# A hybrid decoder step: the samples' first state made in the conv stage, earlier inputs for the scan's first block, the Toeplitz table on other rows

## The chip, the cores and the metric

The kernel runs on one core of a Trainium2 chip. The metric is the device time of one execution in microseconds. The median of three runs stands for the kernel; durations of single steps come from one profiled execution. The engines are called PE (matmul, TensorE), DVE (VectorE), ACT (ScalarE), POOL (GpSimd) and SP (SyncE, which only issues transfers here); POOL issues transfers too.

## What is computed

One step of a two-layer decoder over 256 prompt positions and 8 samples, 264 columns (T) in all. Layer one is a gated short convolution, layer two an S5 state-space layer, and a final RMSNorm follows. In the second layer (D_INNER 4096 as 256 groups of 16, state of 64 complex numbers per group):

```python
proj = h @ w_in
u, z = jnp.split(proj, 2, axis=-1)
lam_bar = jnp.exp(lam * dt)
b_bar = ((lam_bar - 1.0) / lam)[..., None] * b_c
bu = jnp.einsum('tbgh,gph->tbgp', u_c, b_bar)
bu = bu.at[0].add(lam_bar * carry)      # carry: state from before
_, states = lax.associative_scan(_scan_combine, (a_elems, bu), axis=0)
y_c = jnp.real(jnp.einsum('ghp,tbgp->tbgh', c_c, states))
...
y = y + d_skip * uf
y = jax.nn.gelu(y)
y = y * jax.nn.sigmoid(y @ w_glu + b_glu)
out = (y * jax.nn.silu(z)) @ w_out
```

For the samples, `carry` is the given state, so their new state is lam_bar times it plus one `bu`. For the prompt it starts at zero. The new states are outputs.

## The kernel before

All large products run on PE as 640 **slots** of 24 matmuls: eight contraction tiles of 128 by three products. Weights and inputs are split in a high part (wh on ACT, L196; the input's s, L258) and a remainder (wl on DVE, L205; the input's l, L259); a slot computes wh·s, wh·l and wl·s (L230, L231, L233). Slots 0 to 255 are conv's input projection, 256 to 319 its output, 320 to 383 u and 384 to 447 z of the S5 layer, 448 to 575 the GLU, 576 to 639 the last projection. A weight load (raw, L187, on SP) serves two slots; there are three raw buffers, four of wh, three of wl.

The S5 layer works on four blocks q of 64 groups (GB), each in eight tiles of inputs, that is four pairs:

- In conv's stage `tables` and `table_chunks` build, for 32 chunks j, tables from lam, B and C: vt (inputs to states), yt (states to outputs) and tt (a small Toeplitz kernel that takes four positions' inputs straight to their outputs, with d_skip on its diagonal). They go to DRAM as vt_d, yt_d, tt_d. The narrow matmuls of tt are L644, its DVE steps L651 and L655.
- `v_proc` makes bu of a block with vt (L904) and loads the samples' states h0_d into the block's S. `scan_proc` then makes 63 scan steps (L942 to L947, five DVE operations of 128x64, four positions per step). While it scans, the flag `scanning` is set, and wl of slots in the S5 projection is cut into four pieces that stand between the steps' operations (L202, `pop_fill`). After the last step come five operations over 128x512, L956 to L964: lam_bar times the samples' states is added to their bu (`fin`).
- `tw_proc` makes the outputs of each pair: 32 matmuls with tt on the inputs (L1028) and 32 with yt on the states (L1032), a "table pair" below. ACT copies them to yo (L1042), ten transfers write yo to y_d, five on POOL and five on SP (L1050, L1053), SP loads them back as yb (L1056), and ACT makes the gelu (L1058). yb is the GLU's input; the four splits of a tile pair follow (L258, L259).
- `state_out` transposes the block's last states (L978) and writes them out, for the last block on SP ahead of the last yb load (L990, L992).

The GLU's first slots, 448 to 465, are three output pairs with contraction quarters 0 to 2, and 466 to 471 their last quarter. It needs the y of the last block, its last eight contraction tiles 24 to 31, from four pairs. 

The order on each engine is what a planner writes out: `run.go` goes slot by slot, runs `procs` (generators that wait whole slots, or `Lag` microseconds of a counted time, 2.7 per slot) and `sides` (DVE work, by a credit of microseconds per slot). `U_ST` is the lag from the write of u to its use, `tw_done` counts finished pairs and gates the reuse of buffers.

Of the kernel before, what the change touches and what calls it, by code (L numbers as in the profile page):

```python
# [21 lines left out]
NS = 8  # L22
# [102 lines left out]
def tile_hybrid_conv_s5_step(  # L125
# [37 lines left out]
    tt_d = dram.tile([KI, 128, 4, 64], F32, name="tt_d")  # L163
    bp_d = dram.tile([128, G, GS], F32, name="bp_d")
    cp_d = dram.tile([128, G, GS], F32, name="cp_d")
    h0_d = dram.tile([128, G // GB, NS // 2, GB, 2], F32, name="h0_d")
# [31 lines left out]
    def conv_l(i):  # L198
        if i < len(run.slots):
            m = run.slots[i]["m"]  # L200
            wls[i] = wsp.tile([128, 8, 128], F32R, name="wl", bufs=3)
            parts = (4 if scanning[0] else 2) if n_ssm <= i < n_glu else 1  # L202
# [204 lines left out]
    def second_stage():  # L407
# [24 lines left out]
    def tables(pr):  # L432

        lamT, Ft, dcol, msk, eye = (tabs[k] for k in ("lam", "F", "dcol", "msk", "eye"))
# [7 lines left out]
        dr = pr.tile([128, 2, GS], F32, name="dr")  # L442
        mq.dma_start(dr, d_skip.rearrange("o (j gl h) -> (o j) gl h", gl=2, h=GS))
        ev = ident.rearrange("p (a h s) -> p a s h", a=2, h=GS)
        P.tensor_copy(eye, ev[:, 0])
        yield 6
        V.tensor_tensor(eye, eye, ev[:, 1], op=add)
        V.tensor_reduce(msk, eye, axis=mybir.AxisListType.X, op=add)
        drr = pr.tile([128, 2, GS, LC], F32, name="drr")
        P.tensor_copy(drr, dr[:, :, :, None].to_broadcast([128, 2, GS, LC]))  # L450
# [5 lines left out]
        PE.transpose(ps[:, :128], drr.rearrange("j a h s -> j (a h s)"), ident)  # L456
        yield 1
        V.tensor_copy(dcol, ps[:, :128])
# [114 lines left out]
        for k in range(1, 5):  # L573
            yield from spread(lr[k], li[k], lamT[:, :, k - 1, :])
        P.tensor_copy(lam1, lamT[:, :, 0, :])
        P.tensor_copy(lam4, lamT[:, :, 3, :])
# [48 lines left out]

    def table_chunks(ck):

        lamT, Ft, dcol, msk, eye = (tabs[k] for k in ("lam", "F", "dcol", "msk", "eye"))
# [9 lines left out]
        def products(j, X0, Y, vt):  # L638
            mq.dma_start(yt_d[j], Y[:, :, 1:5, :])
            mq.dma_start(vt_d[j], vt)  # L640
            pk = pss.tile([128, 512], F32, name="ps_a")
            pkv = pk[:, :256].rearrange("p (q n) -> p q n", q=4)
            for g in range(8):
                PE.matmul(pkv[(g % 2) * 64:(g % 2) * 64 + 64, g // 2, :],  # L644
                          X0[:, g].rearrange("p h s -> p (h s)"),
                          Y[:, g, 0:4, :].rearrange("p s h -> p (s h)"), start=True, stop=True)
            return pkv

        def toeplitz(j, pkv):
# [12 lines left out]
        prev = None
        for j in range(KI):
# [21 lines left out]
            X0 = ck.tile([128, 8, GS, LC], F32, name="X0")  # L685
# [584 lines left out]
```

## Time and profile before

| | |
|---|---|
| median of 3 runs | 2063.71 us (2061.16 to 2063.89) |
| the profiled execution | 2066.43 us, span 2064.7 us |
| PE busy | 2028.7 us, 98% of the span |
| DVE busy | 1486.7 us, 72% |
| ACT busy | 945.9 us, 46% |
| POOL busy | 198.0 us, 10% |

A busy share is an average over stages. With PE busy for nearly the whole span, one reads where it waits and for whom, then looks at that place in the windows (busy time of each engine per stretch and PE's granted clock) and in the timelines (start and duration of each instruction; in square brackets the idle time ahead of it and what ended that).

### The profile page before, as it was taken

The numbers are of one execution on the slowest core, as the hardware profiler recorded it, in microseconds if no ns is written. First come the engines' busy times: TensorE is split into PE (matmuls) and PEld (weight loads), VectorE is DVE, ScalarE is ACT, GpSimd is POOL, SyncE is SP. The second block draws the span as 40 slices with busy tenths as digits, with TensorE's granted clock in tenths as the row PEclk, the third lists the DMA queues.
The fourth block names the chain that finished last, engine by engine and source line by source line (L and its number), as shares of the span: only waits on it lengthen the run. The fifth ranks groups of instructions, "written<-read, shape, count | busy, mean of one in ns | idle before, by whom it ended". The sixth has DMA issues, their size and how long they took to land. (4 is left out here: it accounts for less than half of the span.)

```text
span 2064.7 us, 44611 instructions
## 1 busy us (share of the span) xinstructions
PE 2028.7 (98%) x17844; PEld 2001.1 (97%) x17844; DVE 1486.7 (72%) x3818; ACT 945.9 (46%) x1417; POOL 198.0 (10%) x365
## 2 busy tenths in 40 slices
PE   9999999999999999999999999999889999999997
PEld 9999999999999999999999999999779999999997
DVE  6785557999999999655548989999835555566453
ACT  6447554444444444444443334444344444455443
POOL 2000000000000000000132252524110000000000
PEclk9999999999999999999999999999989999999998
DMA  8656777776776777766787788879566566655653
GB/s 271 195 186 202 233 233 219 212 216 200 237 215 204 230 219 214 233 202 194 214 275 233 225 244 279 267 240 298 164 184 194 187 191 196 194 186 184 195 179 108
DMA packets 445172, 441.36 MB, mean 214 GB/s; under 512 B 69914, under 2 KB 426252, under 8 KB 444428
## 3 DMA queue, kind: packets, MB, share of 16 engines
q1 hardware_dynamic: 427780, 395.62, 62.4%
q0 software_dynamic: 17152, 42.88, 6.5%
q8 instruction: 140, 2.29, 0.4%
q14 instruction: 68, 0.56, 0.1%
q10 hardware_dynamic: 32, 0.01, 0.0%
HBM read 391.42 MB, written 47.15 MB: 212 GB/s over the span
## 5 line engine op out<-in xcount | busy, mean ns | idle before, releaser
L230 PE MATMUL acc_ps<-s,wh 128*128 128x264 f32 x4544 | 1307.2, 288 | 10.1 <-ACT s L258 8.3
L233 PE MATMUL acc_ps<-s,wl 128*128 128x264 f32 x4528 | 1287.8, 284 | 4.2 <-DVE wl L205 4.2
L205 DVE TENSOR_TENSOR wl<-raw,wh 128x1024 fp32r<-128x1024 f32 (+2 forms) x960 | 826.1, 865 | 369.9 <-PE acc_ps L233 222.7
L196 ACT ACTIVATE wh<-raw 128x1024 fp32r<-128x1024 f32 x640 | 677.7, 1060 | 902.3 <-PE acc_ps L231 709.0
L230 PEld LDWEIGHTS acc_ps<-s,wh 128*128 128x128 f32 x4544 | 858.0, 189 | 17.2 <-ACT s L258 9.4
L231 PE MATMUL acc_ps<-s,wh 128*128 128x264 f32 x3072 | 870.7, 284 | 0.0
L233 PEld LDWEIGHTS acc_ps<-s,wl 128*128 128x128 f32 x4528 | 852.1, 188 | 6.2 <-DVE wl L205 6.1
L231 PEld LDWEIGHTS acc_ps<-s,wh 128*128 128x128 f32 x3072 | 579.3, 189 | 0.0
L231 PE MATMUL acc_ps<-l,wh 128*128 128x264 f32 x1472 | 421.2, 286 | 2.3 <-DVE l L259 2.2
L231 PEld LDWEIGHTS acc_ps<-l,wh 128*128 128x128 f32 x1472 | 278.7, 189 | 3.5 <-DVE l L259 3.5
L943 DVE STREAM_SHUFFLE S<-S 128x64 f32<-128x64 f32 x252 | 74.8, 297 | 0.0
L230 PE MATMUL acc_ps<-yb,wh 128*128 128x264 f32 x256 | 73.0, 285 | 0.0
L230 PE MATMUL acc_ps<-ya,wh 128*128 128x264 f32 x256 | 72.9, 285 | 0.0
L231 PE MATMUL acc_ps<-yb,wh 128*128 128x264 f32 x256 | 72.7, 284 | 0.0
L233 PE MATMUL acc_ps<-ya,wl 128*128 128x264 f32 x256 | 72.6, 284 | 0.0
L233 PE MATMUL acc_ps<-yb,wl 128*128 128x264 f32 x256 | 72.5, 283 | 0.0
L231 PE MATMUL acc_ps<-ya,wh 128*128 128x264 f32 x256 | 72.5, 283 | 0.0
L725 POOL MEMSET ue<- 128x2 f32 x32 | 4.0, 128 | 606.4 <-DVE cv L737 551.8
L947 DVE TENSOR_TENSOR S<-S,prod 128x64 f32<-128x64 f32 x252 | 55.9, 222 | 2.3
L942 DVE TENSOR_TENSOR prod<-S,lam 128x64 f32<-128x64 f32 x252 | 55.5, 220 | 1.9
L945 DVE TENSOR_TENSOR prod<-S,lam 128x64 f32<-128x64 f32 x252 | 56.9, 226 | 0.0
L944 DVE TENSOR_TENSOR S<-S,prod 128x64 f32<-128x64 f32 x252 | 56.3, 223 | 0.0
(321 smaller groups left out, 1791.0 us busy)
## 6 DMA issues: line engine op xcount, KB each, us to landing
raw<-in_conv_w_in_dram SPq DMA_DIRECT2D x127, 1024.0 KB, 6.3
raw<-in_ssm_w_in_dram SPq DMA_DIRECT2D x64, 1024.0 KB, 6.8
raw<-in_ssm_w_glu_dram SPq DMA_DIRECT2D x64, 1024.0 KB, 5.1
raw<-in_conv_w_out_dram SPq DMA_DIRECT2D x32, 1024.0 KB, 5.6
raw<-in_ssm_w_out_dram SPq DMA_DIRECT2D x32, 1024.0 KB, 5.2
yt_d<-Y SPq DMA_DIRECT2D x32, 256.0 KB, 7.1
vt_d<-vt SPq DMA_DIRECT2D x32, 256.0 KB, 6.9
vt<-vt_d POOLq DMA_DIRECT2D x16, 512.0 KB, 7.5
```

Of the source, the lines that this page charges most:

```text
L196: A.activation(whs[i], raws[i][:, :, m * 128:(m + 1) * 128], AF.Copy)
L205: run.fill(lambda k=k: V.tensor_tensor(wls[i][:, k], raws[i][:, k, m * 128:(m + 1) * 128], whs[i][:, k], op=sub))
L230: PE.matmul(ps, wh[:, k, :], H(kt), start=first, stop=False)
L231: PE.matmul(ps, wh[:, k, :], L(kt), start=False, stop=False)
L233: PE.matmul(ps, wl[:, k, :], H(kt), start=False, stop=last)
L725: P.memset(halves(0)[:, :, 0:1], 0.0)
L942: V.tensor_tensor(pr[:, 0], cur, a4[:, 0], op=mult)
L943: V.stream_shuffle(sh, cur, SWAP)
L944: V.tensor_tensor(nxt, nxt, pr[:, 0], op=add)
L945: V.tensor_tensor(pr[:, 1], sh, a4[:, 1], op=mult)
L947: V.tensor_tensor(nxt, nxt, pr[:, 1], op=add)
```

## The change

- `step_samples` runs in conv's stage, after the tables' constants. For each block it loads h0_d, multiplies by lam_bar (shuffle, two products, sum) and writes lh_d. `scan_proc` loads lh when a block's scan begins and does one addition after the last step.
- U_ST is 4 instead of 6, `tw_done` is set one slot earlier, a `yield 1` is gone from `v_proc`, and wl may be cut in four in the GLU too while the scan runs.
- The Toeplitz products of a chunk write groups of 32 rows. The kernel's 16 rows are kept once, with zeros behind them (kt); the Toeplitz form arises in the transfers to tt_d, which read overlapping windows of 64 from it, eight transfers per chunk on POOL instead of one on SP. The five DVE steps become two small ones and a copy on ACT. tt is loaded in pieces of 256 B instead of 1 KB. yt's rows run in reverse, so yo's rows and the lam table do too (not shown).

```diff
-    tt_d = dram.tile([KI, 128, 4, 64], F32, name="tt_d")
+    tt_d = dram.tile([KI, 8, GS, LC, 64], F32, name="tt_d")
...
+    lh_d = dram.tile([128, G // GB, NS // 2, GB, 2], F32, name="lh_d")
...
-            parts = (4 if scanning[0] else 2) if n_ssm <= i < n_glu else 1
+            parts = 4 if scanning[0] else 2 if n_ssm <= i < n_glu else 1
...
             if left[0] == 0:
+                yield from step_samples(pr)
...
+    def step_samples(pr):
+
+        shape = [128, NS // 2, GB, 2]
+        for q in range(NB):
+            gs = slice(q * GB, (q + 1) * GB)
+            bc = lambda k: lam1[:, k, None, gs, None].to_broadcast(shape)
+            h, hs = (pr.tile(shape, F32, name=f"bn{c}") for c in range(2))
+            mq.dma_start(h, h0_d[:, q])
+            yield 4
+            V.stream_shuffle(hs, h, SWAP)
+            yield 0.7
+            V.tensor_tensor(hs, hs, bc(1), op=mult)
+            yield 0.7
+            V.tensor_tensor(h, h, bc(0), op=mult)
+            yield 0.7
+            V.tensor_tensor(h, h, hs, op=add)
+            yield 0.7
+            mq.dma_start(lh_d[:, q], h)
+
...
+            pkv = pk[:, :128].rearrange("p (r n) -> p r n", r=2)
             for g in range(8):
-                PE.matmul(pkv[(g % 2) * 64:(g % 2) * 64 + 64, g // 2, :],
-                          X0[:, g].rearrange("p h s -> p (h s)"),
-                          Y[:, g, 0:4, :].rearrange("p s h -> p (s h)"), start=True, stop=True)
+                PE.matmul(pkv[(g % 4) * 32:(g % 4) * 32 + 32, g // 4, :],
+                          X0[:, g].rearrange("p d h -> p (d h)"),
+                          Y[:, g, 1:5, :].rearrange("p s h -> p (s h)"), start=True, stop=True)
             return pkv
 
         def toeplitz(j, pkv):
-            tt = ck.tile([128, 4, 64], F32, name="tt")
-            V.tensor_tensor(tt, eye.rearrange("p s h -> p (s h)")[:, None, :].to_broadcast([128, 4, 64]),
-                            dcol[:, 4 * j:4 * j + 4, None].to_broadcast([128, 4, 64]), op=mult)
-            yield 0.33
-            for s in range(LC):
-                V.scalar_tensor_tensor(tt[:, :, 16 * s:], pkv[:, :, :64 - 16 * s], msk[:, s:s + 1],
-                                       tt[:, :, 16 * s:], op0=mult, op1=add)
-                yield 0.35 - 0.07 * s
-            mq.dma_start(tt_d[j], tt)
-
+            kt = kts[j % 2]
+            for r in range(2):
+                V.scalar_tensor_tensor(kt[:, r, 48:64], eye, dcol[:, 2 * j + r:2 * j + r + 1], pkv[:, r, 48:64], op0=mult, op1=add)
+            A.activation(kt[:, :, 0:48], pkv[:, :, 0:48], AF.Copy)
+            yield 1
+            for g in range(4):
+                for r in range(2):
+                    w = kt[32 * g:32 * g + GS, r, 0:64]
+                    P.dma_start(tt_d[j, 4 * r + g],
+                                bass.AP(tensor=w.tensor, offset=w.offset, ap=[w.ap[0], [GS, LC], [1, 64]]))
+
+        kts = [ck.tile([128, 2, 112], F32, name=f"kt{i}") for i in range(2)]
+        for kt in kts:
+            P.memset(kt[:, :, 64:], 0.0)
         nxt = load(0)
         yield 3
...
-            X0 = ck.tile([128, 8, GS, LC], F32, name="X0")
-            A.activation(X0, X[:, :, :, 3:4].to_broadcast([128, 8, GS, LC]), AF.Copy)
+            X0 = ck.tile([128, 8, 2, GS], F32, name="X0")
+            A.activation(X0, X[:, :, None, :, 3].to_broadcast([128, 8, 2, GS]), AF.Copy)
...
             while q >= 2 and tw_done[0] < (q - 1) * TB // 2:
                 yield 1
             mq.dma_start(S[:, 0:NS // 2], h0_d[:, q])
-            yield 1
             v_done[0] = q + 1
 
     def v_evac(S, ps, g):
...
+            lh = sw.tile([128, NS // 2, GB, 2], F32, name="lh", tag="big", bufs=1)
+            mq.dma_start(lh, lh_d[:, q])
...
             fin = S[:, a:a + n8]
-            sh8 = sw.tile([128, n8, GB, 2], F32, name="sh8", tag="big", bufs=1)
-            bc = lambda h: lam1[:, h, None, gs, None].to_broadcast([128, n8, GB, 2])
-            V.stream_shuffle(sh8, S[:, 0:n8], SWAP)
-            yield 0.6
-            V.tensor_tensor(sh8, sh8, bc(1), op=mult)
-            yield 0.6
-            V.tensor_tensor(fin, fin, sh8, op=add)
-            yield 0.6
-            V.tensor_tensor(sh8, S[:, 0:n8], bc(0), op=mult)
-            yield 0.6
-            V.tensor_tensor(fin, fin, sh8, op=add)
+            V.tensor_tensor(fin, fin, lh, op=add)
             fin_done[0] = q + 1
...
-        so = sw.tile([128, 4, 2, SD], F32, name="so", tag="big", bufs=1)
+        so = sw.tile([128, 4, 2, SD], F32, name="so", bufs=1)
...
             tt = ss["sw"].tile([128, 2, 4, 64], F32, name="tt", bufs=T_BUFS)
-            sq.dma_start(tt, tt_d[two].rearrange("j p q n -> p j q n"))
+            sq.dma_start(tt, tt_d[two].rearrange("j (q g) h s n -> (g h s) j q n", g=2))
...
                 run.extra += 2.0
                 for g in range(2):
                     spawn(tw_evac(i, yo, g, ps[g]), 1)
-                yield 2
+                yield 1
                 tw_done[0] = i + 1
+                yield 1
         spawn(state_out(NB - 1, S), 2)
 
     def tw_evac(i, yo, p, ps):
...
-    V_BUFS, Y_POOL, U_ST = 2, 5, 6.0
+    V_BUFS, Y_POOL, U_ST = 2, 5, 4.0
```

Some places at which the order of instructions changes. On DVE, the end of the last block's scan; wl is a weight remainder, S1 the block's states. Before:

```order
L942 TENSOR_TENSOR prod_19974<-S1_12666,lam4_76 128x64
L943 STREAM_SHUFFLE S1_12666<-S1_12666 128x64
L944 TENSOR_TENSOR S1_12666<-S1_12666,prod_19974 128x64
L945 TENSOR_TENSOR prod_19974<-S1_12666,lam4_76 128x64
L947 TENSOR_TENSOR S1_12666<-S1_12666,prod_19974 128x64
L1093 TENSOR_TENSOR zt_19721<-zt_19721,yb32_12662 128x264
L205 TENSOR_TENSOR wl_19983<-raw_19763,wh_19940 128x1024
L956 STREAM_SHUFFLE sh8_20009<-S1_12666 128x512
L958 TENSOR_TENSOR sh8_20009<-sh8_20009,lam1_77 128x512
L205 TENSOR_TENSOR wl_20051<-raw_19846,wh_19981 128x1024
L960 TENSOR_TENSOR S1_12666<-S1_12666,sh8_20009 128x512
L962 TENSOR_TENSOR sh8_20009<-S1_12666,lam1_77 128x512
```

After, the same place:

```order
L964 TENSOR_TENSOR prod_19992<-S1_12828,lam4_76 128x64
L965 STREAM_SHUFFLE S1_12828<-S1_12828 128x64
L966 TENSOR_TENSOR S1_12828<-S1_12828,prod_19992 128x64
L967 TENSOR_TENSOR prod_19992<-S1_12828,lam4_76 128x64
L206 TENSOR_TENSOR wl_19959<-raw_19676,wh_19904 128x256
L969 TENSOR_TENSOR S1_12828<-S1_12828,prod_19992 128x64
L206 TENSOR_TENSOR wl_19959<-raw_19676,wh_19904 128x256
L976 TENSOR_TENSOR S1_12828<-S1_12828,lh_18473 128x512
L206 TENSOR_TENSOR wl_20004<-raw_19782,wh_19957 128x256 x4
```

The step now has quarters of wl in it, and one addition with lh follows where five wide operations did; before, 23 steps stood behind the first four GLU splits, after, 12.

On SP, the end of the last block: y_d are the pairs' outputs, yb their loads, so and sp the state outputs. Before:

```order
L187 DMA raw_20393<-in_ssm_w_glu_dram 128x8x256
L1056 DMA yb32_12662<-y_d_83 128x2x264
L1050 DMA y_d_83<-yo_20299 16x8x8
L1053 DMA y_d_83<-yo_20299 16x8x64 x4
L1050 DMA y_d_83<-yo_20395 16x8x8
L1053 DMA y_d_83<-yo_20395 16x8x64 x4
L1056 DMA yb32_12662<-y_d_83 128x2x264
L990 DMA out_4_dram<-sp_20463 64x64
L992 DMA out_6_dram<-so_20462 64x4x64 x2
L990 DMA out_5_dram<-sp_20463 64x64
L992 DMA out_7_dram<-so_20462 64x4x64 x2
L1056 DMA yb32_12662<-y_d_83 128x2x264
```

After:

```order
L188 DMA raw_20500<-in_ssm_w_glu_dram 128x8x256
L1063 DMA y_d_83<-yo_20394 16x8x8
L1066 DMA y_d_83<-yo_20394 16x8x64 x4
L188 DMA raw_20569<-in_ssm_w_glu_dram 128x8x256
L1069 DMA yb32_12824<-y_d_83 128x2x264
L188 DMA raw_20650<-in_ssm_w_glu_dram 128x8x256
L1002 DMA out_4_dram<-sp_20573 64x64
L1004 DMA out_6_dram<-so_20572 64x4x64 x2
L1002 DMA out_5_dram<-sp_20573 64x64
L1004 DMA out_7_dram<-so_20572 64x4x64 x2
L1069 DMA yb32_12824<-y_d_83 128x2x264
```

Two raw loads (for slots 470 and 472) now stand between the last pair's writes and its load; the state outputs are ahead of that load in both. The table pairs of this block stand ahead of slots 453, 455, 458 and 460 on PE now, before ahead of 458, 460, 464 and 466.

On POOL, conv's stage; ue is a channel tile with its halo. Before:

```order
L725 MEMSET ue_3585 128x2
L725 MEMSET ue_3630 128x2
L725 MEMSET ue_4165 128x2
L725 MEMSET ue_4204 128x2
L725 MEMSET ue_4790 128x2
L725 MEMSET ue_4842 128x2
```

After:

```order
L675 DMA tt_d_86<-kt0_4877 64x1x64 x8
L675 DMA tt_d_86<-kt1_4878 64x1x64 x8
L746 MEMSET ue_8647 128x2
L675 DMA tt_d_86<-kt0_4877 64x1x64 x8
L746 MEMSET ue_8707 128x2
L675 DMA tt_d_86<-kt1_4878 64x1x64 x8
```

Groups of eight transfers of the table now stand between the memsets of conv's channels.

## Rows read from the trace of the kernel before

**Rows 1.** PE's waits for other engines: us in total, times, longest.

```profile
PE acc_ps L230 <- ACT s L258: 8.3, 4, 2.6
PE ps_a L978 <- DVE prod L942: 0.8, 1, 0.8
```

**Rows 2.** Windows of 10 us, columns: us, each engine's busy time, PEclk, DMA share, GB/s.

```profile
1450.00:1460.00 10.00, 7.15 (x52) 6.52 (x53) 9.79 (x40) 4.12 (x7) 0.00 (x0) 1.00 0.44 149
...
1520.00:1530.00 10.00, 4.44 (x17) 3.25 (x15) 1.55 (x4) 3.87 (x11) 0.00 (x0) 0.58 0.42 99
```

**Rows 3.** PE timeline, slots 448, 458, 462, 463, 464, within 466, 467, 468.

```profile
1442.98 0.28 PE L230 MATMUL acc_ps<-s,wh 128*128 128x264 f32 x1
...
1485.64 0.59 PE L230 MATMUL acc_ps<-s,wh 128*128 128x264 f32 x1
...
1500.33 0.28 PE L230 MATMUL ps_a<-s,wh 128*128 128x264 f32 x1
...
1503.25 0.28 PE L230 MATMUL ps_a<-s,wh 128*128 128x264 f32 x1
...
1508.13 0.39 PE L230 MATMUL ps_a<-s,wh 128*128 128x264 f32 x1
...
1530.78 0.59 PE L230 MATMUL acc_ps<-s,wh 128*128 128x264 f32 x1 [2.61 <-ACT s L258]
...
1532.52 0.42 PE L230 MATMUL acc_ps<-s,wh 128*128 128x264 f32 x1
...
1536.68 0.29 PE L230 MATMUL acc_ps<-s,wh 128*128 128x264 f32 x1
```

**Rows 4.** DVE timeline at the last scan: quarter pieces, splits, whole piece, last step's end.

```profile
1425.04 0.22 DVE L942 TENSOR_TENSOR prod<-S,lam 128x64 f32<-128x64 f32 x1
...
1425.65 0.42 DVE L205 TENSOR_TENSOR wl<-raw,wh 128x256 fp32r<-128x256 f32 x1
...
1426.46 0.22 DVE L942 TENSOR_TENSOR prod<-S,lam 128x64 f32<-128x64 f32 x1
...
1439.27 1.46 DVE L259 TENSOR_TENSOR l<-yb,s 128x264 fp32r<-128x264 f32 x4
...
1440.65 1.22 DVE L205 TENSOR_TENSOR wl<-raw,wh 128x1024 fp32r<-128x1024 f32 x1
...
1443.67 1.46 DVE L259 TENSOR_TENSOR l<-yb,s 128x264 fp32r<-128x264 f32 x4
...
1483.61 0.43 DVE L1093 TENSOR_TENSOR zt<-zt,yb 128x264 f32<-128x264 f32 x1
```

**Rows 5.** ACT timeline: the last gelu.

```profile
1529.63 0.64 ACT L1058 ACTIVATE yb<-yb 128x528 f32<-128x528 f32 x1 [3.14 <-DMA yb<-y_d]
```

**Rows 6.** SP timeline: last y_d writes, state outputs, last yb load.

```profile
1518.42 3.64 SPq L1053 DMA_DIRECT2D y_d<-yo  x4
...
1522.79 0.50 SPq L990 DMA_DIRECT2D out_dram<-sp  x1
...
1526.81 0.41 SPq L1056 DMA_DIRECT2D yb<-y_d  x1
```

**Rows 7.** Groups by shape, DVE: busy, mean ns.

```profile
L956 DVE STREAM_SHUFFLE sh<-S 128x512 f32<-128x512 f32 x4 | 3.0, 742 | 0.0
```

**Rows 8.** PE timeline: one group of the table's narrow matmuls.

```profile
358.44 0.69 PE L644 MATMUL ps_a<-Y,X 128*64 128x64 f32 x16
```

**Rows 9.** Line L1053, ns min/median/max, its POOL half.

```profile
L1053 POOL DMA_DIRECT2D y_d<-yo x64: 531/531/548, 1202.6 to 1519.1; - x64
```

**Rows 10.** DMA issues: KB each, median us to landing.

```profile
uct<-u_d POOLq DMA_DIRECT2D x16, 256.0 KB, 6.0
tt<-tt_d POOLq DMA_DIRECT2D x16, 256.0 KB, 6.6
```

**Rows 11.** The page's costliest groups: conv's memset on POOL.

```profile
L725 POOL MEMSET ue<- 128x2 f32 x32 | 4.0, 128 | 606.4 <-DVE cv L737 551.8
```

More of the change, by code (lines that the diff above doesn't have):

```diff
@@ L412, in second_stage @@
         tabs["F"] = tb.tile([128, 2, 4, G], F32, name="Ft")
-        tabs["dcol"] = tb.tile([128, 128], F32, name="dcol")
-        tabs["msk"] = tb.tile([128, LC], F32, name="msk")
-        tabs["eye"] = tb.tile([128, LC, GS], F32, name="eye")
+        tabs["dcol"] = tb.tile([128, 64], F32, name="dcol")
+        tabs["eye"] = tb.tile([128, GS], F32, name="eye")
         pre_p = tc.tile_pool(name="pre", bufs=1)
@@ L432, in tables @@
     def tables(pr):
-        lamT, Ft, dcol, msk, eye = (tabs[k] for k in ("lam", "F", "dcol", "msk", "eye"))
+        lamT, Ft, dcol, eye = (tabs[k] for k in ("lam", "F", "dcol", "eye"))
         nt = lambda name: pr.tile([128, 2, SD], F32, name=name)
@@ L441, in tables @@
         mq.dma_start(ldr, log_dt.rearrange("o (a g) -> (o a) g", a=2))
[L442 to L450, printed above, removed]
+        dr = pr.tile([64, 4, GS], F32, name="dr")
+        mq.dma_start(dr, d_skip.rearrange("o (j g h) -> (o j) g h", g=4, h=GS))
+        yield 2
+        V.tensor_reduce(eye, ident.rearrange("p (a h) -> p h a", h=GS), axis=mybir.AxisListType.X, op=add)
+        drr = pr.tile([64, 4, 2, GS], F32, name="drr")
+        P.tensor_copy(drr, dr[:, :, None, :].to_broadcast([64, 4, 2, GS]))
         ps = pss.tile([128, 512], F32, name="ps_a")
@@ L455, in tables @@
         ps = pss.tile([128, 512], F32, name="ps_a")
-        PE.transpose(ps[:, :128], drr.rearrange("j a h s -> j (a h s)"), ident)
+        PE.transpose(ps[:, :64], drr.rearrange("j g d h -> j (g d h)"), ident[:64, :64])
         yield 1
-        V.tensor_copy(dcol, ps[:, :128])
+        V.tensor_copy(dcol, ps[:, :64])
         M = 12582912.0
@@ L573, in tables @@
         for k in range(1, 5):
-            yield from spread(lr[k], li[k], lamT[:, :, k - 1, :])
-        P.tensor_copy(lam1, lamT[:, :, 0, :])
-        P.tensor_copy(lam4, lamT[:, :, 3, :])
+            yield from spread(lr[k], li[k], lamT[:, :, 4 - k, :])
+        P.tensor_copy(lam1, lamT[:, :, 3, :])
+        P.tensor_copy(lam4, lamT[:, :, 0, :])
         for k in range(4):
@@ L624, in state_layout @@
             mq.dma_start(h0_d[:, 2 * a2:2 * a2 + 2], ho)
+    def step_samples(pr):
[15 more added lines that the diff above has]
+            mq.dma_start(lh_d[:, q], h)
     def table_chunks(ck):
-        lamT, Ft, dcol, msk, eye = (tabs[k] for k in ("lam", "F", "dcol", "msk", "eye"))
+        lamT, Ft, dcol, eye = (tabs[k] for k in ("lam", "F", "dcol", "eye"))
         full = [128, 8, LC, GS]
@@ L691, in table_chunks @@
             Y = ck.tile([128, 8, 5, GS], F32, name="Y", bufs=2)
-            A.activation(Y[:, :, 0, :], cp, AF.Copy)
-            V.tensor_tensor(Y[:, :, 1:5, :], tab(lamT, 0), row(cp), op=mult)
+            A.activation(Y[:, :, 4, :], cp, AF.Copy)
+            V.tensor_tensor(Y[:, :, 0:4, :], tab(lamT, 0), row(cp), op=mult)
             yield 0.6
@@ L697, in table_chunks @@
             yield 0.6
-            V.tensor_tensor(Y[:, :, 1:5, :], Y[:, :, 1:5, :], m, op=sub)
+            V.tensor_tensor(Y[:, :, 0:4, :], Y[:, :, 0:4, :], m, op=sub)
             yield 0.6
@@ L1049, in tw_evac @@
             dq = P if 5 * jj < Y_POOL else mq
-            dq.dma_start(rows[:, :, NP:], yo[a:a + GS, :, 0:NS])
+            dq.dma_start(rows[:, :, NP:], yo[a + 3 * GS:a + 4 * GS, :, 0:NS])
             for s in range(LC):
                 dq = P if 5 * jj + s + 1 < Y_POOL else mq
-                dq.dma_start(rows[:, :, s * NCH:(s + 1) * NCH], yo[a + s * GS:a + (s + 1) * GS, :, Z:Z + NCH])
+                dq.dma_start(rows[:, :, s * NCH:(s + 1) * NCH], yo[a + (3 - s) * GS:a + (4 - s) * GS, :, Z:Z + NCH])
         yield Lag(Y_ST)
@@ L1087, in glu_in @@
         yield 1
-        sz = ss["sw"].tile([128, T], F32, name="sz", tag="sz" if j < 2 else "tt", bufs=1 if j < 2 else None)
+        sz = ss["sw"].tile([128, T], F32, name="sz", tag="so" if j < 2 else "tt", bufs=1 if j < 2 else None)
         A.activation(sz, zt, AF.Sigmoid)
```

3 lines of the change are left out of this document (1 added, 2 removed).

## Prediction

> **What bounds the kernel now.** I read the page's busy table first: TensorE (PE) is busy nearly all the time, so only time in which PE stands still, or runs at its lower clock, can be won. The list of PE's waits comes second. Its longest entry is the matmuls of L230 that wait for ACT's split of a GLU input [rows 1], all in one place. The table of windows shows what that place looks like: from 1450 to 1460 PE has 7.15 of 10 us with DVE at 9.79, and from 1520 to 1530 PE has 4.44 of 10 us at a granted clock of 0.58, that is between its two levels, 1.2 and 2.4 GHz, after it had stood still [rows 2]. PE's timeline gives the size. An ordinary slot of 24 matmuls takes 1503.25 - 1500.33 = 2.92 us, one with a table pair (L1028, L1032) 1508.13 - 1503.25 = 4.88 us, so the pair is 1.96 us [rows 3]. Slots 448 to 467, the start of the GLU, take 1536.68 - 1442.98 = 93.70 us [rows 3]; twenty slots and four pairs would take 58.4 + 7.8 = 66.2 us. The 27.5 us between are what the change can reach, and they lie in two parts:
>
> - **Scan part**, slots 448 to 457, 1485.64 - 1442.98 = 42.66 us for ten slots and one pair (31.2 us): 11.5 us too much. DVE is the late engine. A round of it (four splits, one weight remainder wl, two scan steps) takes 1443.67 - 1439.27 = 4.40 us against PE's 2.92 [rows 4].
> - **Tail part**, slots 458 to 467, 1536.68 - 1485.64 = 51.04 us for ten slots and three pairs (35.1 us): 15.9 us too much, of which I put 0.6 down to the five transposes of state_out, an estimate from the pair's 1.96 us for 64 matmuls; they stand in both kernels. Here PE waits at slot 466 for the outputs of the last four pairs: yo to y_d, back as yb, through the gelu on ACT. The last gelu waited 3.14 us for the transfer yb<-y_d [rows 5]. That load was issued at 1526.81, behind y_d writes from 1518.42 and the state outputs from 1522.79 on the same queue [rows 6].
>
> **The change part by part.**
>
> *lam_bar times the samples' states.* Per block, five DVE operations of 128x512 (0.742 us for the shuffle [rows 7]) become one; four at 0.74 at most are 3.0 us per block that leave DVE. Four sets of shuffle, two products and a sum go to the conv stage, as do a load of h0_d and a write of lh_d for each on SP; the block then loads lh, 256 KB, on SP. In conv, PE waits for neither DVE nor ACT for longer than the list's small entries, so these 4 x 3.0 = 12 us of DVE lie under PE; without that cover they would cost up to 12 us. At the earlier blocks the add frees state_out sooner: the 0.8 us for which PE waited at L978 [rows 1] goes.
>
> *Sooner inputs.* U_ST goes from 6 to 4, tw_done is set a slot earlier and a yield is gone. By the order of the changed kernel the scan of the last block moves forward against the slots: from the first four splits on, 23 scan steps were left, now 12. The last pairs stand at slots 453, 455, 458 and 460 (before 458, 460, 464, 466). So a pair's result has six slots more before slot 466 needs it.
>
> *Scan part.* The new rounds still hold four splits and one wl, now as four quarters between two steps. Two steps with quarters take 2 x (1426.46 - 1425.04) = 2.84 us and the four splits 1440.65 - 1439.27 = 1.38 [rows 4], so a round is 4.22 us. Six rounds are 25.3 us, against 1483.61 - 1439.27 = 44.3 us from the first four splits to the end of the last step, where the next operation starts [rows 4]: 19.0 us earlier on DVE. But the first pair stands five slots, 14.6 us, earlier on PE. The wait shrinks by 19.0 - 14.6 = **4.4 us**. Bounds: if the four quarters cost their full 0.42 us each in place of the whole piece's 1.22 [rows 4], a round would be 4.40 + 1.68 - 1.22 = 4.86 us, six 29.2, and 15.1 - 14.6 = 0.5 us is won; if the wait vanished, 11.5. I take 4.4, since the steps with quarters were timed in the same scan.
>
> *Tail part.* Let T be the start of slot 466. The pairs are done by slot 460, so all four y_d writes are out before T. What is late next is SP's queue: after raw(472), which waits for wl(467) and thus for PE's end of slot 464 (T - 2.9, plus 1.2 for wl), stand the state outputs, 1526.81 - 1522.79 = 4.0 us [rows 6], and only then yb of the last pair. It is issued at about T - 1.7 + 0.4 + 4.0 = T + 2.7; from there to the gelu took 1529.63 - 1526.81 = 2.8 us [rows 5, 6], and PE went on 1.15 us after that, at 1530.78 [rows 3]. So PE continues at T + 6.7 with the last quarter of a slot that it reaches at T + 2.2: 4.5 us of wait instead of some 13. With 1.2 us for the lower clock behind it (slot 467 took 1536.68 - 1532.52 = 4.16 instead of 2.92 [rows 3]) the excess is 5.7 us instead of 15.3 (15.9 less the transposes): **9.6 us** won. Bounds: 15.3 if the state outputs come out early, 0 if each transfer slips as before.
>
> *Table stage.* On DVE five operations per chunk become two of 128x16, with a copy on ACT: under PE, nothing. Eight matmuls of L644 per chunk write 32 columns of the array instead of 64. A group of sixteen records took 0.69 us [rows 8]. At 2.92 us for 24 matmuls of 264 columns [rows 3], 64 moving columns are 0.030 us, and sixteen one behind the other 0.47; a group in which the two halves overlapped would have had 0.24. I take 0, from the row, since the records stand one behind the other. The table is written by eight POOL transfers of 16 KB per chunk instead of one of SP; POOL takes 0.531 us for each issue [rows 9], so 256 take 136 us, on an engine that is mostly idle. tt is loaded in pieces of 256 B instead of 1 KB: uct, in 256-B pieces, landed in 6.0 us against tt's 6.6 [rows 10], so I take 0.
>
> The Trainium skill, "DMA: Bandwidth & Descriptors" (Specifications and Rules for kernel authors), speaks against this: below 512 B a transfer no longer goes at line rate, and under 64 KB it is mostly overhead. The landing times of uct and tt do not bear it out here; by the rule tt would land later, which U_LAG would hide up to its 8 us.
>
> **The sum.** 4.4 + 9.6 + 0.8 = 14.8 us. The profiled execution took 2066.43 us (span 2064.7), so it would take 2051.6; it lay 2.7 above the median of the three runs, 2063.71, from which I forecast **2048.9 us**.
>
> **The rivals.**
>
> 1. *The tail's wait goes altogether.* yb arrives before its quarter: if the state outputs are issued while PE is still in slot 464, or yb's four loads land early. For: six slots, 17.5 us, of new room, and gelus that are short. Against: SP's order puts raw(472) and the outputs ahead. The 5.7 us of excess that I left go too: 2043.2 us. Chance 0.14.
> 2. *The tail stays nearly as long.* Transfers of yo, yb and the raw loads collide (SP already took 3.64 us to issue four y_d writes in the tail [rows 6], 0.9 each where POOL takes 0.531 [rows 9]), and each yb slips by as much as the pairs came earlier. Then the scan part, the 0.8 us and a little is all: 5.5 us, 2058.2 us. Chance 0.18, a quarter of it within 0.2%.
> 3. *The change does not do what it says.* Only the place of the stall moves: rounds at the bound of 4.86 us win 0.5 us, and the last yb, behind a raw load and state outputs that come as late as ever, wins 3 us at most: 2060 to 2063.7. Chance 0.10.
> 4. *The narrow matmuls overlap.* If four groups of 32 columns ran side by side, the 0.47 us of a group would go to a quarter, 0.12, that is 0.35 us for each of 32 chunks: 11 us more, 2037.7 us; at half that, 2043.3. Against it: in [rows 8] the two halves of before show no overlap. Chance 0.06. The Trainium skill, "TensorE: Matmul & The Clock Gate" (Part 3, Measured speedup vs the span model), has three such column groups at 2.38 times the speed. By that figure, an estimate, the saving would be 0.27 us a group and 8.7 us in all.
> 5. *Slower: POOL holds up the conv stage.* The memset of ue (L725), for which ACT's next copy into ue waits, stands behind the table's transfers on POOL; until now POOL waited there mostly for DVE [rows 11]. One group of eight is 8 x 0.531 = 4.2 us, which the two slots of lead (5.8 us) cover. It decides from two groups in a row: 8.5 us, 2.7 us too late, at each of some ten channel pairs of that stage, 27 us, or 12.2 net: 2075.9 us. Against it: a chunk comes every four to five slots, so two groups seldom meet. Chance 0.10.
>
> **How the numbers follow.** The forecast (2046 to 2053, from the bounds of the quarters and of the outputs) has 0.42. Some 0.2%, 4.1 us, is about what a measurement of this kernel can tell from no change. Faster by more: 0.42 + 0.14 + 0.06 + 0.14 of case 2 = 0.76. Same: 0.04 of case 2 and case 3, 0.14. Slower: 0.10. The range from 2041 to 2061 leaves out case 5, most of case 3 and the far half of case 4.
>
> **What would show it.** Right: PE's slots 448 to 467 take about 80 us, the wait at slot 466 is one of 4 to 5 us and ends with the last yb, which is issued right behind the state outputs; DVE's rounds are 4.2 us until slot 453 and PE has no wait from there to 465; the entry L978<-DVE prod is gone; the conv stage has its old length. Wrong: new waits of PE before slot 446, above all for the channels of conv or for raw (cases 5, 2); a group of the narrow matmuls that takes less than 0.5 us (case 4); waits of over 9 us up to slot 453 (case 3).

## The result and the profile after

The changed kernel takes 2046.26 us (median of 4 runs, 2044.34 to 2047.38), the kernel before, in the same comparison, 2062.43 (4 runs): ratio 0.9919, 95% interval 0.9907 to 0.9932, that is 16.2 us less. The forecast was 2048.9, that is 14.8 less. The profiled execution after took 2047.05 us, span 2045.3.

From the start of each slot in PE's timeline one gets the length of any stage. This table is worked out that way (us):

| slots | stage | before | after | difference |
|---|---|---|---|---|
| 0 to 31 | conv, start | 99.84 | 101.66 | +1.8 |
| 32 to 319 | conv with the table chunks, conv's output | 888.88 | 880.76 | -8.1 |
| 320 to 447 | u and z, the scans | 440.52 | 440.47 | 0.0 |
| 448 to 457 | GLU, scan part | 42.66 | 41.95 | -0.7 |
| 458 to 467 | GLU, tail part | 51.04 | 39.48 | -11.6 |
| 468 to 638 | rest | 508.29 | 508.31 | 0.0 |

The first slot began 0.8 us earlier; with it the sum is the 19.4 us by which the spans differ. The medians differ by 16.2, since the profiled execution of before lay 4.0 us above the median of the four runs and that of after 0.8 us above its own. In the scan part the numbers hide a move: two table pairs more (3.9 us) now stand in it. Without them the scan part won 0.7 + 3.9 = 4.6 us and the tail 11.6 - 3.9 = 7.7, together 12.3.

PE's waits after (us in total, times, longest), against [rows 1], where the wait for ACT's split stood at 8.3 and L978 at 0.8:

```profile
PE acc_ps L231 <- ACT s L259: 3.9, 2, 3.4
PE acc_ps L234 <- DVE wl L206: 2.5, 3, 1.0
...
PE ps_b L1044 <- DVE S L969: 1.3, 1, 1.3
...
PE acc_ps L232 <- DVE l L260: 1.3, 2, 0.6
...
PE ps_a L925 <- ACT S L938: 0.8, 1, 0.8
...
PE ps_a L925 <- DMA u_d<-ut: 0.5, 1, 0.5
PE ps_a L925 <- DMA vt<-vt_d: 0.4, 1, 0.4
```

The wait at state_out of a middle block is not in the list. The matmuls that make bu (L925, before L904) wait 1.7 us in all, before 0.4. The windows (us, busy time of PE, its weight load, DVE, ACT, POOL, granted clock, DMA share, GB/s), against [rows 2]:

```profile
1440.00:1450.00 10.00, 8.20 (x63) 7.56 (x63) 10.00 (x48) 5.53 (x11) 0.00 (x0) 1.00 0.33 106
1450.00:1460.00 10.00, 7.09 (x103) 6.30 (x102) 10.00 (x45) 3.40 (x3) 2.02 (x3) 1.00 0.53 166
1460.00:1470.00 10.00, 10.00 (x131) 9.70 (x130) 5.43 (x9) 4.32 (x8) 7.01 (x12) 1.00 1.04 330
...
1500.00:1510.00 10.00, 6.80 (x52) 6.17 (x50) 4.01 (x6) 4.29 (x8) 0.00 (x0) 0.99 0.70 214
1510.00:1520.00 10.00, 9.18 (x53) 9.00 (x54) 3.92 (x6) 5.19 (x8) 0.00 (x0) 0.67 0.36 118
```

DVE is full up to 1460 with PE at seven to eight tenths, then PE has no gap until slot 466. One stretch of standing still is left around 1510, after which the granted clock is 0.67, between the two levels, as before in [rows 2].

PE's timeline, slots 448, 453, 466, the two places in 466 where it waited, 467 and 468 (the answer to [rows 3]):

```profile
1435.87 0.28 PE L231 MATMUL acc_ps<-s,wh 128*128 128x264 f32 x1
...
1459.10 0.39 PE L231 MATMUL acc_ps<-s,wh 128*128 128x264 f32 x1
...
1503.90 0.29 PE L231 MATMUL acc_ps<-s,wh 128*128 128x264 f32 x1
...
1506.08 0.39 PE L231 MATMUL acc_ps<-s,wh 128*128 128x264 f32 x1 [0.55 <-ACT s L259]
...
1510.82 0.59 PE L231 MATMUL acc_ps<-s,wh 128*128 128x264 f32 x1 [3.39 <-ACT s L259]
...
1512.56 0.42 PE L231 MATMUL acc_ps<-s,wh 128*128 128x264 f32 x1
...
1517.30 0.28 PE L231 MATMUL acc_ps<-s,wh 128*128 128x264 f32 x1
```

Slots 448 to 467 take 1517.30 - 1435.87 = 81.43 us instead of 93.70. DVE's timeline shows the new round and the end of the scan (against [rows 4]):

```profile
1432.79 1.46 DVE L260 TENSOR_TENSOR l<-yb,s 128x264 fp32r<-128x264 f32 x4
...
1437.02 1.46 DVE L260 TENSOR_TENSOR l<-yb,s 128x264 fp32r<-128x264 f32 x4
...
1457.77 0.42 DVE L206 TENSOR_TENSOR wl<-raw,wh 128x256 fp32r<-128x256 f32 x1
1458.10 0.69 DVE L976 TENSOR_TENSOR S<-S,lh 128x512 f32<-128x512 f32 x1
```

A round is 1437.02 - 1432.79 = 4.23 us (forecast 4.22, before 4.40), and the first four splits to the end of the scan are 1458.10 - 1432.79 = 25.3 us, as the sum had it, where it was 44.3. Then comes the one addition. SP's queue (against [rows 6]) and the last gelu on ACT (against [rows 5]):

```profile
1502.46 0.37 SPq L188 DMA_DIRECT2D raw<-in_ssm_w_glu_dram  x1
1502.93 0.54 SPq L1002 DMA_DIRECT2D out_dram<-sp  x1
1503.53 1.27 SPq L1004 DMA_DIRECT2D out_dram<-so  x2
1504.90 0.56 SPq L1002 DMA_DIRECT2D out_dram<-sp  x1
1505.50 1.27 SPq L1004 DMA_DIRECT2D out_dram<-so  x2
1507.00 0.42 SPq L1069 DMA_DIRECT2D yb<-y_d  x1
```

```profile
1509.67 0.64 ACT L1071 ACTIVATE yb<-yb 128x528 f32<-128x528 f32 x1 [3.32 <-DMA yb<-y_d]
```

With T = 1503.90, the last yb is issued at T + 3.1 (forecast T + 2.7) behind raw(472) and the state outputs, is in the gelu 1509.67 - 1507.00 = 2.7 us later, and PE goes on at T + 6.9 (forecast T + 6.7). From there on it runs at the lower of its two levels for a while, as windows of 1 us show (the clock is the third number from the end):

```profile
1510.00:1511.00 1.00, 0.18 (x1) 0.18 (x1) 0.20 (x1) 0.97 (x3) 0.00 (x0) 0.50 0.00 0
...
1515.00:1516.00 1.00, 1.00 (x6) 1.00 (x6) 0.00 (x0) 0.00 (x0) 0.00 (x0) 0.50 0.60 137
...
1517.00:1518.00 1.00, 1.00 (x10) 1.00 (x10) 0.44 (x1) 0.50 (x2) 0.00 (x0) 1.00 1.09 388
```

The last six matmuls of slot 466 and the 24 of slot 467 take 1517.30 - 1510.82 = 6.48 us, where at 2.92 us a slot they would take 3.65.

What the forecast did not have is in the conv stage. One group of the table's narrow matmuls after, against [rows 8], where it took 0.69 us:

```profile
514.08 0.43 PE L661 MATMUL ps_a<-Y,X 128*32 128x64 f32 x16
```

A slot with such a group fell from 3.61 us (median of 32) to 3.35, and one without stayed at 2.90: 0.26 us in each of 32 slots, 8 us. POOL's transfers (all issues of L675, and the median landing of loads in the scans; against [rows 9] and [rows 10]):

```profile
L675 POOL DMA_DIRECT2D tt_d<-kt x256 | 128.9, 525 | 362.6 <-ACT kt L670 320.5
```

```profile
uct<-u_d POOLq DMA_DIRECT2D x16, 256.0 KB, 6.5
tt<-tt_d POOLq DMA_DIRECT2D x16, 256.0 KB, 8.8
...
yt<-yt_d POOLq DMA_DIRECT2D x16, 512.0 KB, 7.9
```

The load of yt, whose pieces did not change, landed sooner before:

```profile
yt<-yt_d POOLq DMA_DIRECT2D x16, 512.0 KB, 6.2
```

POOL spends the 129 us, and where it waited, it was for the table's copy on ACT, not PE for it.

### The profile page after: what moved, and what is told of

Its sections match the earlier page's. It is cut to its first block, busy times and chain, and to the rows that moved or that the text cites. A ratio compares the mean times of both kernels' runs of the same rounds, so it can differ in the third digit from the quotient of the medians.

```text
span 2045.3 us, 45097 instructions
## 1 busy us (share of the span) xinstructions
PE 2015.4 (99%) x17844; PEld 1988.3 (97%) x17844; DVE 1442.0 (71%) x3746; ACT 953.6 (47%) x1449; POOL 328.1 (16%) x622
## 5 line engine op out<-in xcount | busy, mean ns | idle before, releaser
L675 POOL DMA_DIRECT2D tt_d<-kt x256 | 128.9, 525 | 362.6 <-ACT kt L670 320.5
```

The costliest lines, as they stand in the source:

```text
L675: P.dma_start(tt_d[j, 4 * r + g], bass.AP(tensor=w.tensor, offset=w.offset, ap=[w.ap[0], [GS, LC], [1, 64]]))
```

## Experiments

The lengths of stages below are again worked out from PE's timeline. The order of the last block is the same in the changed kernel and in e3 and e8 to e11, and slots 448 to 467 took 79.8 to 82.4 us in these six executions (mean 80.7), slots 320 to 447 between 439.3 and 442.9. What lies within such a spread is not read as an effect. Most of the spread is the place of DVE's first four GLU splits, 2.0 to 4.2 us ahead of slot 448. Counted from these splits to the start of slot 468, the six executions agree within 0.8 us (83.7 to 84.5, mean 84.2); the kernel before takes 97.4.

### e1: the five wide operations back at the end of the scan

```diff
-            lh = sw.tile([128, NS // 2, GB, 2], F32, name="lh", tag="big", bufs=1)
-            mq.dma_start(lh, lh_d[:, q])
...
-            V.tensor_tensor(fin, fin, lh, op=add)
+            V.stream_shuffle(sh8, S[:, 0:n8], SWAP)
+            V.tensor_tensor(sh8, sh8, bc(1), op=mult)
+            V.tensor_tensor(fin, fin, sh8, op=add)
+            V.tensor_tensor(sh8, S[:, 0:n8], bc(0), op=mult)
+            V.tensor_tensor(fin, fin, sh8, op=add)
```

The new tile sh8, the lam_bar broadcast `bc` and the `yield 0.6` behind each operation, as in the kernel before, are left out here.

> The changed kernel with the five wide operations put back at the end of each block's scan (lh_d is still made in conv, but not loaded). Theory A, that the early pairs come from these operations having left the scan's chain: by the order the last block's table pairs go back to slots 457, 459, 462 and 464, some ten instead of six rounds of 4.2 us stand ahead of the first of them, and the last yb is issued about 5 us after slot 466 starts instead of 3.1. Slots 448 to 467 take 87 to 89 us instead of 81.4 and the wait at state_out of a middle block (0.8 us) is back: 2052 to 2054 us. Conv stage as in the changed kernel. Theory B, that the earlier inputs (U_ST 4) and the earlier tw_done bring the gain and the wide operations only cost their own 2.8 us at the end: slots 448 to 467 take 82 to 84 us, 2047 to 2049 us.

Measured: 2052.3 us, ratio 0.9939 (0.9924 to 0.9954); the changed kernel's was 0.9919. Slots 448 to 467 took 85.86 us, 5.2 above the mean of the spread, and the pairs stood where the order says, 457 to 464. That is theory A in mechanism and between the two in size. The wait at state_out of a middle block did not come back. The last yb was issued at 1511.03 with T = 1504.38, at T + 6.65, where about 5 was expected:

```profile
1505.63 0.38 SPq L1077 DMA_DIRECT2D yb<-y_d  x1
1506.10 0.52 SPq L1010 DMA_DIRECT2D out_dram<-sp  x1
...
1511.03 0.42 SPq L1077 DMA_DIRECT2D yb<-y_d  x1
```

### e6 and e7: tw_done and the yield as before, with and without the wide operations

```diff
-                yield 1
+                yield 2
                 tw_done[0] = i + 1
-                yield 1
...
             mq.dma_start(S[:, 0:NS // 2], h0_d[:, q])
+            yield 1
```

e7 has e1's edit besides.

> The changed kernel with tw_done and the yield of v_proc as before; by the order the last pairs then stand at 453, 455, 459 and 461, the state outputs' transposes at 465 instead of 464. Theory A, that the wide operations' leaving is the larger part: slots 448 to 467 take 81.5 to 83 us (changed kernel 81.4). Theory B, that tw_done is: 85 us or more.

> Both taken back: the five wide operations at the end of the scan, tw_done and the yield as before; left of the change are the table's part, U_ST 4 and wl in quarters in the GLU. By the order the pairs stand where they stood before, at 458, 460, 464 and 466. Theory A, that only the pairs' places count: slots 448 to 467 take 91 to 94 us, as before (93.7), less some 2 us for the quarters in ten rounds; the conv stage keeps its 8 us. Theory B, that U_ST or the quarters matter: under 89 us.

Measured: e6 83.30 us in slots 448 to 467 (2050.04 in one run, in which slots 320 to 447 were 5 us longer, 445.5), e7 89.24 (2054.2). So the earlier tw_done is worth 2.6 us against the mean of the spread, near what can be told, and 3.4 us between e7 and e1; the wide operations are worth 5.2 (e1) or 5.9 (e7 to e6). Counted from the first four splits to slot 468, e1 takes 90.1 us, e6 85.6 and e7 93.4: 1.5 or 3.3 us for tw_done with the yield, 5.9 or 7.7 for the wide operations. DVE's timeline shows what moved: behind the first four splits stand 23 steps of the last scan before and in e7, 21 in e1, 14 in e6, and 12 in the changed kernel and in e10. e7 falls between its two theories: with the pairs back at 458 to 466 its tail is as before (slots 464 to 467: 28.29 us, before 28.55), but the scan part is 39.29 instead of 42.66 us. Most of that lies on DVE: the same 23 steps end 42.4 us after the first four splits instead of 44.3 (to the zt operation that follows, as in [rows 4]). Each kernel has six rounds with splits; those of two steps take 4.22 us instead of 4.40, which fits the quarters.

### e2 and e10: whole wl in the GLU; U_ST 6

```diff
-            parts = 4 if scanning[0] else 2 if n_ssm <= i < n_glu else 1
+            parts = (4 if scanning[0] else 2) if n_ssm <= i < n_glu else 1
```

```diff
-    V_BUFS, Y_POOL, U_ST = 2, 5, 4.0
+    V_BUFS, Y_POOL, U_ST = 2, 5, 6.0
```

> The changed kernel with wl cut in four only up to slot 447, whole in the GLU as before. My theory: a round of DVE goes from 4.22 to 4.40 us, six rounds, so 1 us more in slots 448 to 453 and nothing elsewhere: slots 448 to 467 take 82.5 us instead of 81.4, time 2046 to 2048 us. Rival: the quarters let the scan's steps through sooner than the rounds tell and are worth the scan part's gain of some 4 us: 85 to 86 us, 2050 us.

> The changed kernel with U_ST at 6 as before. By the order only the first inputs of a block move by a slot, the table pairs stay. Theory, that this part of the change is worth nothing: slots 448 to 467 take 81 to 83 us, slots 320 to 447 the 438 to 445 us that they show in the other runs, time as the changed kernel's within 2 us. Rival, that the scan depends on it: the last scan's rounds reach two slots further, 448 to 467 at 84 us or more.

Measured: e2 82.65 us in slots 448 to 467 and 2048.36 us, ratio 0.9920 (0.9903 to 0.9937), not to be told from the changed kernel. Its rounds are 4.39 us again, and from the first splits to slot 468 it takes 86.6 us, 2.5 more than the mean. By that count the quarters are worth more than the 1 us that was expected; the medians do not show it. e10 79.80 us and 2045.38 (one run): the earlier inputs of a block, which the change is named after, are worth nothing that shows.

### e3, e8 and e9: what made the conv stage shorter

e3: 64 columns again, at two positions, one half of each stationary operand zero (the zeroed operands and their two copies on ACT are not shown).

```diff
-                PE.matmul(pkv[(g % 4) * 32:(g % 4) * 32 + 32, g // 4, :],
+                PE.matmul(pkv[(g % 4) // 2 * 64:(g % 4) // 2 * 64 + 64, g // 4, :],
...
-                          Y[:, g, 1:5, :].rearrange("p s h -> p (s h)"), start=True, stop=True)
+                          Y[:, g, 1:5, :].rearrange("p s h -> p (s h)"), start=g % 2 == 0, stop=g % 2 == 1)
```

> The changed kernel with matmuls of the table's chunk writing 64 array columns at two positions again, half of each stationary operand being zero, so the result and the number of matmuls stay. Theory, that the 8 us which the conv stage lost come from the narrower matmuls alone: a slot with such a group goes from 3.35 back to 3.61 us, 32 groups, 8 us, time 2053 to 2055 us, all of it between slots 110 and 290. Rival, that the conv stage got faster since DVE has less to do there or SP's queue is freer: the slot stays at 3.35 to 3.4 and the time within 2 us of the changed kernel's 2046.3.

Measured: 2054.32 us, ratio 0.9946 (0.9932 to 0.9961). Slots 112 to 287 took 552.76 us instead of 543.03 (before 550.44), and a slot with a group 3.66 instead of 3.35 (before 3.61). The form of the matmuls alone carries the 8 us of conv, with 2.3 us on top in e3. Is it their width, or that groups of columns work side by side?

```diff
-            for g in range(8):
+            for g in (0, 4, 1, 5, 2, 6, 3, 7):
```

> The changed kernel with the eight matmuls of a table group in the order 0, 4, 1, 5, 2, 6, 3, 7, so that two in a row write the same 32 columns of the array. If the narrow matmuls got cheaper since four groups of columns work side by side, two neighbours on the same columns come one behind the other and a slot with a group goes from 3.35 to some 3.5 us, 4 to 8 us in all. If only the width counts (32 columns to load and to write instead of 64), the slot stays at 3.35 us and the conv stage keeps its length.

Measured: a slot with a group 3.38 us, conv stage 543.65 (2044.02 us in one run). Two neighbours on the same columns cost 0.03 us, which spoke for the width alone. e9 then put all eight on the same columns. DVE clears the bank ahead of them (not shown), and what follows reads only the first pieces of it, so the rest of the Toeplitz table is left out:

```diff
-                PE.matmul(pkv[(g % 4) * 32:(g % 4) * 32 + 32, g // 4, :],
+                PE.matmul(pk[0:32, g * 64:g * 64 + 64],
```

> The changed kernel with all eight matmuls of a table group writing the same 32 array columns, into eight pieces of the bank that DVE has cleared before; what follows reads only the first pieces, so the Toeplitz table, and the second layer with it, is not computed rightly; the amount of work stays. If groups of columns work side by side, which e8 speaks against, none can here and a slot with such a group takes 3.6 us or more, 8 us in all. If the price goes by the width of the stationary operand alone, the slot stays at 3.35 to 3.4 us, and the conv stage (slots 112 to 288) at 543 us.

Measured: a slot with a group 4.00 us, slots 112 to 287 574.15 us, 31 longer (2073.15 us in one run). The groups are 21 of these, 0.65 us each; the other 10 lie in six slots from 256 to 281, where PE waited for that clearing (5.5 us) and for ACT. The group in PE's timeline, of e9 and of e8:

```profile
501.02 1.08 PE L660 MATMUL ps_a<-Y,X 128*32 128x64 f32 x16
```

```profile
496.96 0.45 PE L661 MATMUL ps_a<-Y,X 128*32 128x64 f32 x16
```

At equal width, 1.08 us on one group of columns against 0.43 on four: groups of columns do work side by side, and the width alone is refuted. Beyond a slot of 2.90 us, one position costs 1.10, two 0.71 (before) to 0.76 (e3), four 0.45. How many records of a group start together can be read too. Here is PE's timeline cut off 0.07 us behind the start of a group, for the kernel before, the changed one, e8 and e9:

```profile
358.44 0.28 PE L644 MATMUL ps_a<-Y,X 128*64 128x64 f32 x2
```

```profile
514.08 0.26 PE L661 MATMUL ps_a<-Y,X 128*32 128x64 f32 x4
```

```profile
496.96 0.28 PE L661 MATMUL ps_a<-Y,X 128*32 128x64 f32 x4
```

```profile
501.02 0.24 PE L660 MATMUL ps_a<-Y,X 128*32 128x64 f32 x1
```

Two records start together on two positions, four on four, one on one; in e9 the sixteen starts are spread over 0.86 us, 0.057 apart. In e8 four start together as well, so its order costs next to nothing. How they do, with neighbours on the same columns, no run shows.

### e11: the table's transfers twice

```diff
-                    P.dma_start(tt_d[j, 4 * r + g],
+                    for t in (tt_d, tt_e):
+                        P.dma_start(t[j, 4 * r + g],
```

> The changed kernel with each of the eight POOL transfers of a chunk made twice, the second to a place that nothing reads: 16 issues, 8.1 us of POOL per chunk of 15.5 us. By case 5 of the prediction the memsets of conv's channels, with two slots of lead, come up to 2.3 us late: waits of PE on conv's channels, conv stage (slots 112 to 288) 5 to 20 us longer than 543. By the traces so far, in which POOL's transfers cost nothing, the lead may be larger: conv stage within 1 us.

Measured: slots 112 to 287 543.02 us, 2044.87 us in one run. POOL has more idle time to give in conv than even twice the change's load needs; case 5 was far from its point.

### e4, e5 and e12: the queue ahead of the last yb

e4 gives the last block's state outputs to POOL. e5 has that and an earlier yb load, e12 the earlier load alone.

```diff
+            oq = P if q == NB - 1 else mq
-            mq.dma_start(dp[0, 0, gs, :], sp[:, c, :])
+            oq.dma_start(dp[0, 0, gs, :], sp[:, c, :])
```

```diff
-    U_LAG, Y_ST, Y_LD, T_BUFS = 8.0, 11.0, 10.0, 2
+    U_LAG, Y_ST, Y_LD, T_BUFS = 8.0, 6.0, 10.0, 2
```

> The changed kernel with the last block's state outputs issued by POOL instead of SP. Theory, that SP's queue sets the last wait: yb of the last pair is issued right after raw(472), 1 us before slot 466 starts instead of 3.1 us after it; the wait for the last split falls from 3.4 us to under 1 us (then ACT's two gelus in a row and the one for the pair before set it), the cold clock after it goes as well: slots 448 to 467 take 76 to 78 us instead of 81.4, time 2041 to 2043 us. Rival, that the landing of the y_d writes sets it: yb's load waits on the queue for them, the wait stays above 2.5 us, time 2045 to 2047.

> As e4 (state outputs on POOL), and the lag between the writes of y_d and the load of yb is 6 instead of 11 us, which by the order puts the last yb load ahead of raw(472) and the gelu before it ahead of wh(469). Theory, that in e4 the load landed late (5.7 us after its issue instead of 2.7) since 1 MB of raw(472) had been put on the transfer engines 0.7 us before it: now the load is issued about 2 us before slot 466 starts or earlier and lands in 3 us, PE's waits in slot 466 fall from 3.1 to under 1 us together, slots 448 to 467 take 75 to 77 us (e4: 80.3), time 2038 to 2041 us. Rival, that SP now stands at the yb loads until the y_d writes have landed, and the raw loads behind them come late: a new wait for wh or wl of slots 460 to 470, 448 to 467 at 79 us or more, time 2043 or more.

> The changed kernel with the lag ahead of the yb loads at 6 instead of 11 us and the state outputs left on SP. By the order the last yb load now stands ahead of raw(472) and of the state outputs. Theory, that only the place of this load on SP counts: slots 448 to 467 take 74 to 76 us as in e5 (74.4), time as e5's 2036 us within 2 us. Rival, that POOL taking over the outputs did part of it (raw(474) behind them is late by 4 us otherwise): 76 us or more, a wait for wh or wl at slots 470 to 476, time 2039 us or more.

Measured: e4 2044.31 us, ratio 0.9902 (0.9883 to 0.9922), slots 464 to 467 17.65 us against 18.5 to 19.3 in the runs of the same order. Slots 448 to 467 took 80.31 us, where 76 to 78 were expected. The wait for the last split is 2.56 us, as the rival had it, but not for the rival's reason, since the load did not stand on the queue. SP and ACT of e4:

```profile
1501.60 0.37 SPq L188 DMA_DIRECT2D raw<-in_ssm_w_glu_dram  x1
1502.32 0.36 SPq L1070 DMA_DIRECT2D yb<-y_d  x1
```

```profile
1507.98 0.64 ACT L1072 ACTIVATE yb<-yb 128x528 f32<-128x528 f32 x1 [2.50 <-DMA yb<-y_d]
```

The load was issued 0.7 us ahead of T (1503.04) instead of 3.1 behind it, but the gelu came 5.7 us after the issue instead of 2.7: 1 MB of raw weights had gone out 0.7 us ahead of it. In e5 and e12 it goes out ahead of raw(472). SP of e12, where T is 1500.83, and the landing of that load:

```profile
1493.03 0.39 SPq L188 DMA_DIRECT2D raw<-in_ssm_w_glu_dram  x1
1494.35 0.38 SPq L1069 DMA_DIRECT2D yb<-y_d  x1
1499.41 0.37 SPq L188 DMA_DIRECT2D raw<-in_ssm_w_glu_dram  x1
1499.84 0.58 SPq L1002 DMA_DIRECT2D out_dram<-sp  x1
```

```profile
yb<-y_d SPq DMA_DIRECT2D x1, 264.0 KB, 6.0
```

It was issued 6.5 us ahead of T. It took about as long to land as in e4, here with raw(470) 1.3 us ahead of it, but it was there 0.5 us before T. Slots 464 to 467 take 12.21 us in both, which is four slots and 0.5 us of transposes, with no wait; slots 448 to 467 take 74.4 us in e5 and 73.5 in e12. e5 takes 2036.33 us, ratio 0.9862 (0.9840 to 0.9884), e12 2036.44, ratio 0.9864 (0.9847 to 0.9880). Both beat both kernels, and e12 shows that the earlier yb loads alone do it: 27.5 us below before.

## Why the prediction was right, and where it was not

- **Scan part.** Right: rounds of 4.23 us, 25.3 us to the end of the scan, 4.6 us won against a forecast of 4.4, no wait of PE between 453 and 465, the pairs at the slots that the order gives. Named wrongly was what moved them: U_ST is worth nothing (e10: still 12 steps); of the 11 steps by which the scan moved, the five wide operations are 9 (21 in e1, 12 without them) and tw_done with the yield is 2 (14 in e6). The prediction had counted the wide operations only as 3.0 us per block that leave DVE.
- **Tail part.** Right in mechanism and nearly in size: raw(472), the state outputs and then yb, PE's two waits 0.55 and 3.39 us, going on at T + 6.9. The tail won 7.7 us, not 9.6. The term that was mis-sized is the clock behind the wait: slots 466 and 467 took 1517.30 - 1503.90 = 13.4 us, 7.6 above two slots of 2.92, where I had 4.5 + 1.2 = 5.7. PE went on at T + 6.9 instead of T + 2.2, so the waits took 4.7; the other 2.8 are the 30 matmuls behind them (6.48 us instead of 3.65), in a stretch with a granted clock of 0.50. Slot 467, from which I took the 1.2, lost 1.8 of these; the end of slot 466 lost the rest and was not in the sum. Together, slots 448 to 467 won 12.3 us in the profile (13.0 by the mean of six), against 14.0. Rival 1, that the wait goes altogether, did not come by itself; e12 is that case, 7.2 us less in these slots than the mean of six.
- **state_out's 0.8 us.** The wait is gone, but slots 320 to 447 took as long as before: the waits of L925 there are 1.7 us instead of 0.4, and the spread of that stage, some 4 us, is larger than the term. The reason that I gave, the shorter end of the scan, is not borne out: in e1 and e7 the wide operations are back and this wait is not. What removed it stays open.
- **The table's matmuls.** Here the step failed. I took 0 because sixteen records in 0.69 us looked like sixteen one behind the other at 0.030 us each, a pitch taken from the wide matmuls. On one position they take 1.08 (e9), so the halves of before did overlap, as the two records that start together there show, and four groups took 8 us off. That is rival 4, to which I gave 0.06, with a bound of 11 us. Its price by the figure of the Trainium skill ("TensorE: Matmul & The Clock Gate", Part 3, Measured speedup vs the span model), 8.7 us, was nearer. That is luck: both prices start from 0.47 us for a group without overlap, which takes 1.08, while the change went from two positions to four, 0.69 to 0.43 us. Four groups against one are 1.08 / 0.43 = 2.5 times here.
- **Sum.** 12.3 + 8.1 in the parts that moved, less 1.8 us in the start, which in other runs of the same code took 100.1 to 101.7, and plus the 0.8 us by which the first slot began earlier, is the 19.4 us of the spans. Part of that is the profiled execution of before, which ran a little slower also where both kernels do the same (slots 496 to 575: 235.20 us, in all other kernels 234.1). So the total came out within 3 us partly by luck, since a term put at zero and two that were a little too large, the tail and state_out, made up for each other.
- **Rivals 2, 3 and 5.** The tail did shrink, the stall did not merely move, and POOL held up nothing (e11). The tt loads landed in 8.8 us instead of 6.6, issue 0.90 instead of 0.72 us, so the 0 taken from [rows 10] was wrong. The Trainium skill ("DMA: Bandwidth & Descriptors", Specifications) has transfers in pieces under 512 B below line rate, and the direction agrees. How much of the delay comes from the pieces of 256 B no run shows, since yt, which kept its pieces, also landed 1.7 us later and uct 0.5. As forecast nothing waits for tt on PE.

## What to carry to other kernels

Price a small matmul from a row of the same type and width in the same trace, and never from wide ones of another type: the length of the whole group hid an overlap that was already there, and the timeline cut off just behind its start shows it. Where a queue carries both large loads and the one small transfer that the bound engine waits for, its issue and its landing both count: behind a large load it landed 5.7 to 6.0 us after its issue instead of 2.7. Taking away only part of what stood ahead of it (e4) won a third at most of what issuing it 6.5 us ahead of its slot won (e12), though it landed as slowly there. A lag in a planner that nobody has priced (U_ST here, Y_ST) can be worth nothing or 10 us: the order tells which slot it moves before any run does.

## What the runs showed of the hardware

- Matmuls of f32 with 64 moving columns, sixteen records to a group: 1.08 us on one group of 32 array columns (e9), 0.69 on two of 64 (before), 0.43 on four of 32, 0.45 with neighbours on the same columns (e8).
- A 264 KB load on SP was used 2.7 us after its issue with 1 MB issued 4.5 us ahead on the same queue (changed kernel), and 5.7 us after it with 1 MB issued 0.7 us ahead (e4); with 1 MB 1.3 us ahead it landed in 6.0 us (e12).
- 256 or 512 transfers of 16 KB from POOL beside a DVE that is busy half of the time and more took 0.52 to 0.53 us of POOL each, and the conv stage was as long with 512 as with 256 (e11).
- At the end of a wait of 3.39 us PE's granted clock was 0.50 and stayed there while it worked on, up to 1516 us; the 30 matmuls behind the wait took 6.48 us instead of 3.65 (changed kernel).
